# One fixed instruction order for the attention units of a hybrid attention and linear-attention block

## The chip, the cores and the metric

One core of a Trainium2 chip runs the whole kernel in one launch. The metric is the device time in microseconds (us). TensorE (PE) multiplies and transposes into PSUM; VectorE (DVE), ScalarE (ACT) and GpSimd (POOL) do the elementwise work; SyncE (SP) and here also ACT issue DMAs. The program lists each engine's instructions in an order of its own, and semaphores hold an instruction until what it needs is there.

## The reference

One layer of an encoder, 512 positions by 2048 channels in float32:

```python
mod = silu(c) @ w_cond + b_cond;  shift, scale, gate = split(mod, 3)
proj = (rms_norm(x) * (1 + scale) + shift) @ w_in       # 2048 x 7200
aq, ak, av, ag, gq, gk, gv, gg, lr_f, lr_b = split(proj)
a_out = attention(aq, ak, av) * silu(ag)   # 16 heads x 64, three dilated windows + bias, merged
g_o = gla(gq, gk, gv, log_g_f) + flip(gla(flipped, log_g_b))   # 4 heads, dk 128, dv 256
g_out = rms_norm(g_o) * gain * silu(gg)
x = x + gate * (concat(a_out, g_out) @ w_out)
return rms_norm(x) * final_gain
```

The kernel computes the three windows of a head as one softmax over all 512 keys, with a bias row that holds mask, multiplicity and relative position.

## The kernel before

A float32 operand is split into a high part (rounded to float32r, by ACT) and a low part (the difference, by DVE); `three` makes a product of three float32r matmuls (hi*hi, hi*lo, lo*hi). So every group of weights costs one ACT and one DVE pass over 128x1024 before PE can use it (`split_hi`, `split_lo`; the tiles are named qk42h and qk42l for group 2 of unit qk4).

The input projection runs in units of 512 columns: first two that are planned together with the loading of the inputs (sa, sb), then qk2, qk4, qk6 (queries and keys of head pairs 2 to 7), gk, gv0, gv1, ag0, ag1, gg0, gg1, and the output projection o0 to o3. A unit has 8 groups of weights; for each it makes 6 matmuls for each of its four tiles, 24 in all, into four PSUM banks of the pool `pj` (5 banks; the other three, pool `pa`, serve scores, transposes and values). A "tick" is 3 matmuls, a unit has 64. Beside the matmuls a unit carries side work: a list of (place, function), where the place is a share of the unit's ticks; what lies at 1 or above goes to the next unit at its place less one ("spill").

In qk2, qk4, qk6 and gk the side work is the attention of two head pairs whose queries and keys were made one unit earlier: 16 tiles (4 heads by 4 blocks of 128 queries), each of them
- `score`: two matmuls into s, then on DVE p = min with the bias and the row's extreme (`tensor_tensor_reduce`, L580), on ACT the exponential with the row's sum (L583), on DVE the reciprocal (L584), on POOL the scaling (L585);
- `turn`: four PE transposes of p into t, then ACT's high part (L601) and DVE's low part (L602) into pt;
- `values`, for every two tiles: eight matmuls of pt with v into o, an ACT copy oh and a DVE addition into cat.

The places are spread evenly from 0.17 over 0.8 of the unit (`ATT_AT`), transposes behind the score of two tiles later. After a unit `qk_evict` takes the new queries and keys out of the four banks, for each pair: ACT writes qs and ks, DVE their low parts (qs, kl), and SP copies ks and kl to the other 64 partitions by DMA.

PE's order is the order of the source (`manual_schedule(engines={E.PE})`). The other engines' instructions are ordered by the framework's scheduler from its own estimates, except in the start, where the block that plans the inputs lists them (`PLANNED`). In some units DVE also does "half sums" (`some_sums`, L244 and L680: 1024 columns of a weight matrix with one row, from a 512 KB load), as many as `SUMS_IN` says. Weight loads, half-sum loads and bias loads (`g_load`) all go over SP's queue. The names raw, rawv and rawg stand for loads that share four buffers.

Of the kernel before, what the change touches and what calls it, by code (L numbers as in the profile page):

```python
# [18 lines left out]
P = 128  # L19
# [114 lines left out]
def block_kernel(ctx: ExitStack, tc: tile.TileContext, a: dict):  # L134
# [15 lines left out]
    def B8(name, shape, dt=F32):  # L150
        return b8.tile([P] + shape, dt, tag="b8", name=name)
# [140 lines left out]
    def split_lo(i):  # L292
        if i in raws and i not in low:
            u, g = groups[i]
            raw = raws[i].rearrange("p k c -> p (k c)")
            hi, lo = wts[i]
            tt(lo, raw, hi.bitcast(F32), op=ALU.subtract)
            low.add(i)
# [257 lines left out]
    def attention(pairs):  # L556

        tiles = [(2 * p + j, i) for p in pairs for j in range(2) for i in range(4)]
        gt, pt, pr_ = {}, {}, {}
        heads = [2 * p + j for p in pairs for j in range(2)]  # L560

        def g_load(h):
            g = gp.tile([P, 896], F32, tag="g", name=f"g{h}")
            nc.sync.dma_start(g, bass.AP(grow.tensor, grow.offset + h * 1024, [[1, P], [1, 896]]))
            gt[h] = g

        def score(h, i):
            def go():
                if h % 8 == 0 and i == 0:
                    cat[h // 8] = B8(f"cat{h // 8}", [4, 512])  # L570
# [5 lines left out]
                mm(ps, qs[:, q], ks, start=True, stop=False)  # L576
                mm(ps, qs[:, q], kl, start=False, stop=True)  # L577
                t = T2(f"p{h}{i}")
                st = sm.tile([P, 3], F32, tag="st", name=f"st{h}{i}", bufs=6)
                nc.vector.tensor_tensor_reduce(  # L580
                    out=t, in0=ps, in1=gt[h][:, P * i:P * i + 512], op0=ALU.add, op1=ALU.min,
                    scale=1.0, scalar=3e38, accum_out=st[:, 0:1])
                act(t, t, AF.Exp, bias=st[:, 0:1], scale=-1.0, accum_out=st[:, 1:2])  # L583
                nc.vector.reciprocal(st[:, 2:3], st[:, 1:2])  # L584
                nc.gpsimd.tensor_scalar(t, t, st[:, 2:3], 1.0, op0=ALU.mult, op1=ALU.mult)  # L585
                pr_[h, i] = t
            return go

        def turn(h, i):
            def go():  # L590
                half, ii = divmod(i, 2)
                if ii == 0:
                    pt[h, half] = B8(f"pt{h}{half}", [2, 4, 256], F32R)
                t = pr_.pop((h, i))
                pk = PA(f"t{h}{i}")
                for kt in range(4):
                    nc.tensor.transpose(pk[:, kt * P:kt * P + P], t[:, kt * P:kt * P + P], ident)  # L597
                hi = pt[h, half][:, 0, :, P * ii:P * ii + P]
                lo = pt[h, half][:, 1, :, P * ii:P * ii + P]
                src = pk.rearrange("p (k q) -> p k q", k=4)  # L600
                act(hi, src, AF.Copy)  # L601
                tt(lo, src, hi.bitcast(F32), op=ALU.subtract)  # L602
            return go

        def values(h, half):
            def go():
                t = pt.pop((h, half))
                po = PA(f"o{h}{half}")
                for kt in range(4):
                    for w in range(2):  # L610
                        mm(po[:, :256], vv[h // 4][:, kt, h % 4, :], t[:, w, kt, :],  # L611
                           start=kt == 0 and w == 0, stop=kt == 3 and w == 1)
# [10 lines left out]
        for x in range(n + 4):  # L623
            if x < n:
                items.append(score(*tiles[x]))
            if 2 <= x <= n + 1:
                items.append(turn(*tiles[x - 2]))
            if 3 <= x <= n + 2 and tiles[x - 3][1] % 2 == 1:
                items.append(values(tiles[x - 3][0], tiles[x - 3][1] // 2))
        g_load(heads[0])  # L630
        start, span, move0, move1, move_last = ATT_AT
        at = [start + (q + 0.5) / len(items) * span for q in range(len(items))]
        at[0] -= move0
        at[1] -= move1
        at[-1] += move_last
        return list(zip(at, items))

    def gate_half(m, z):

# [203 lines left out]
    def unit(name, natural, side=(), rhs=None, lr=None, tiles=range(4)):  # L843
# [5 lines left out]
        for q in range(KT // 2):  # L849
            g = gorder[q] if name == "o3" else q  # L850
            i0 = gi[name, g]
            todo = []
            if 0 in tiles:
                todo = list(range(gi[name, gorder[0] if name == "o3" else 0], upto[name, g] + 1))
                for i in todo:
                    split_hi(i)
                for ahead in (1, 2):
                    fetch(upto[name, g] + ahead)
            if i0 not in low:
                split_lo(i0)  # L860
            hi, lo = wts[i0]
            for n, i in enumerate(tiles):
                for kk in range(2):
                    k = 2 * g + kk
                    rh, rl = (h_hi[:, k, :], h_lo[:, k, :]) if rhs is None else rhs[k]
                    if natural:
                        t = slice(i * P, i * P + P)
                        cw = slice(kk * 512, kk * 512 + 512)
                        three(ps[n], rh[:, t], rl[:, t], hi[:, cw], lo[:, cw], q + kk == 0, q + kk == KT // 2)
                    else:  # L870
                        c = slice(kk * 512 + i * P, kk * 512 + i * P + P)
                        three(ps[n], hi[:, c], lo[:, c], rh, rl, q + kk == 0, q + kk == KT // 2)
                    tick += 1
                    if tick % (2 * len(tiles)) == 2:
                        for i_ in todo:
                            split_lo(i_)
                    while pos < len(side) and side[pos][0] * ticks <= tick:
                        urgent(side[pos][1])
                        pos += 1
                if lr is not None:  # L880
                    lr(4 * g + i)
            for i_ in todo:
                split_lo(i_)
        while pos < len(side):
# [12 lines left out]
        lnexp()  # L897


    for p in range(2):  # L900
        qk_evict(p, psb["b", 4 + 2 * p], psb["b", 5 + 2 * p])
    for n, p in (("qk2", 0), ("qk4", 2), ("qk6", 4)):
        ps = unit(n, False, attention((p, p + 1)) + ([(0.05, shift_row)] + some_sums(n) if p == 4 else []))
        for q in range(2):
            qk_evict(p + 2 + q, ps[2 * q], ps[2 * q + 1])

    ps = unit("gk", False, attention((6, 7)) + some_sums("gk"))
    gla["k"] = B8("gkt", [4, 512])
    for i in range(4):
        act(gla["k"][:, i, :], ps[i], AF.Copy)  # L910


    lrb = B8("lrb", [KT, 32])
    nc.sync.dma_start(lrb, a["w_lr"][0])
    lrs = B8("lrs", [KT, 2, 32], F32R)
    act(lrs[:, :, 0, :], lrb, AF.Copy)
    tt(lrs[:, :, 1, :], lrb, lrs[:, :, 0, :].bitcast(F32), op=ALU.subtract)
    plr = PA("plr")

    def lr_tick(n):  # L920
        if n % 2 == 1:
            k = n // 2
            w = lrs[:, k, :, :].rearrange("p a b -> p (a b)")
            mm(plr[:64], w, h_hi[:, k, :], start=k == 0, stop=False)
            mm(plr[:64], w, h_lo[:, k, :], start=False, stop=k == KT - 1)

    ps = unit("gv0", True, some_sums("gv0"), lr=lr_tick)
    gla["v0"] = B8("gv0", [4, 512])
    for i in range(4):
        act(gla["v0"][:, i, :], ps[i], AF.Copy)  # L930
# [200 lines left out]
```

## Time and profile before

| | |
|---|---|
| three runs | 958.09, 958.55, 958.55 us; median 958.55 |
| the profiled execution | 959.9 us; its span (first to last instruction) 957.9 us |
| granted TensorE clock | 0.997 |
| busy | PE 98%, DVE 63%, ACT 45%, POOL 8% of the span |
| stage of the four attention units | about 192 to 460 us |

A line of instructions reads: start, duration, engine, source line, operation, what it writes and reads, and in brackets the engine's idle time before it and what ended it. Matmuls overlap, so the pace is the distance of their starts. A line of waits reads: who waited for whom, us in total, times, longest.

### The profile page before, as it was taken

The page shows a single profiled execution, that of the slowest core. Times are in us where ns is not written, and L with a number is a line of the kernel's source. Part 1 is how long each engine was busy: PE and PEld are TensorE (multiplying, and loading weights), DVE is VectorE, ACT ScalarE, POOL GpSimd, SP SyncE. Part 2 cuts the span into 40 slices and gives each one's busy share as a digit, 9 for nine tenths or more (in the row PEclk, how much of TensorE's full clock was granted, in tenths as well). Part 3 has the DMA queues.
Part 4 walks back from the last instruction along what each step waited for, and adds up shares of the span by engine and source line. Part 5 has one row for each costly group of instructions (what it writes and reads, how often), then busy time and mean ns, then how long its engine had stood idle before and what let it go on. Part 6 is the DMA issues. An engine that isn't in the chain of part 4 may idle for free.

```text
span 957.9 us, 11999 instructions
## 1 busy us (share of the span) xinstructions
PE 939.7 (98%) x4464; PEld 777.1 (81%) x4464; DVE 605.3 (63%) x900; ACT 431.5 (45%) x719; POOL 81.1 (8%) x100
## 2 busy tenths in 40 slices
PE   8999999999999999999999999999999999999996
PEld 5888788888888888888778888888887888888884
DVE  7988899675756676766435656675964352546421
ACT  5443533565655655655215544543834152233222
POOL 0000000012122022122000000000010000202120
PEclk9999999999999999999999999999999999999998
DMA  9999687443333463533454244354555464244013
GB/s 330 413 411 365 229 296 275 150 131 105 112 103 105 144 200 108 173 127 103 150 176 146 86 132 154 132 176 154 173 195 183 132 221 154 92 151 152 23 55 121
DMA packets 45180, 163.76 MB, mean 171 GB/s; under 512 B 5730, under 2 KB 6018, under 8 KB 40386
## 3 DMA queue, kind: packets, MB, share of 16 engines
q1 hardware_dynamic: 44946, 162.68, 49.9%
q8 instruction: 35, 0.57, 0.2%
q10 hardware_dynamic: 176, 0.33, 0.1%
q14 instruction: 23, 0.18, 0.1%
HBM read 154.51 MB, written 4.28 MB: 166 GB/s over the span
## 4 chain that ended last, share of the span: by engine, by line
PE 84%; DMA 6%; DVE 5%; issue 3%; ACT 1%; SPq 0%; POOL 0%; ACTq 0%; DVEq 0%; POOLq 0%
PE ps_o L170 6%; PE ps_o L169 6%; PE ps_o L171 6%; DMA rawg<-in_wg 6%; PE ps_qk L170 5%; PE ps_qk L169 5%; PE ps_qk L171 5%; PE o L611 3%; PE sta L169 3%; PE sta L170 3%; PE sta L171 3%; PE stb L171 3%; PE stb L169 3%; PE stb L170 3%; PE ps_gv L171 3%; PE ps_gv L170 3%
## 5 line engine op out<-in xcount | busy, mean ns | idle before, releaser
L585 POOL TENSOR_SCALAR p<-p,st 128x512 f32<-128x512 f32 x64 | 45.5, 711 | 406.6 <-DVE st L584 357.9
L244 DVE CUSTOM_DVE_ANT_0 cb<-cb,sb,c_bcond 128x2048 f32<-128x2048 f32 (+1 forms) x32 | 73.4, 2294 | 0.0
L583 ACT ACTIVATE p<-p,st 128x512 f32<-128x512 f32 x64 | 46.1, 721 | 56.8 <-DVE st L580 56.3
L602 DVE TENSOR_TENSOR pt<-t,pt 128x512 fp32r<-128x512 f32 x64 | 44.0, 689 | 16.2 <-ACT pt L601 15.8
L580 DVE CUSTOM_DVE_ANT_0 p<-s,g 128x512 f32<-128x512 f32 x64 | 43.6, 687 | 14.8 <-PE s L577 14.5
L601 ACT ACTIVATE pt<-t 128x512 fp32r<-128x512 f32 x64 | 37.8, 592 | 10.2 <-PE t L597 9.2
L244 DVE CUSTOM_DVE_ANT_0 rawg<-rawg,sb,gate 128x1024 f32<-128x1024 f32 x16 | 20.5, 1283 | 29.6 <-DMA rawg<-in_wg 29.6
L611 PEld LDWEIGHTS o<-pt,vv 128*128 128x128 f32 x256 | 34.7, 188 | 5.0 <-DVE pt L602 2.2
L597 PEld LDWEIGHTS t<-c_ident,p 128*128 128x128 f32 x256 | 31.8, 140 | 8.5
L597 PE MATMUL t<-c_ident,p 128*128 128x128 f32 x256 | 38.3, 272 | 0.0
L611 PE MATMUL o<-pt,vv 128*128 128x256 f32 x256 | 36.6, 283 | 0.9 <-DVE pt L602 0.8
L244 DVE CUSTOM_DVE_ANT_0 rawg<-rawg,sb,c_bcond 128x1024 f32<-128x1024 f32 x16 | 20.5, 1283 | 26.3 <-DMA rawg<-in_wg 26.3
L1014 POOL TENSOR_TENSOR x<-x,fgain 128x512 f32<-128x512 f32 x12 | 20.3, 1696 | 185.3 <-ACT ysq L1012 185.3
L1012 ACT ACTIVATE ysq<-x 128x512 f32<-128x512 f32 x16 | 10.1, 632 | 47.2 <-DVE x L1010 47.2
L767 POOL TENSOR_SCALAR dc<-st,sc 128x256 f32<-128x256 f32 x16 | 10.4, 652 | 245.5 <-DVE st L764 240.6
L1009 DVE TENSOR_TENSOR y<-ps_o,sb 128x512 f32<-128x512 f32 x16 | 10.9, 684 | 25.9 <-PE ps_o L171 25.9
L584 DVE RECIPROCAL st<-st 128x1 f32<-128x1 f32 x64 | 10.3, 162 | 24.9 <-ACT p L583 24.9
L576 PE MATMUL s<-ks,qs 128*128 128x512 f32 x64 | 25.1, 391 | 0.0
L577 PE MATMUL s<-kl,qs 128*128 128x512 f32 x64 | 25.0, 391 | 0.0
L774 ACT ACTIVATE sq<-st,sc 128x256 f32<-128x256 f32 x24 | 12.2, 509 | 26.8 <-DVE st L769 14.3
L1010 DVE TENSOR_TENSOR x<-y,x 128x512 f32<-128x512 f32 x16 | 18.0, 1125 | 0.3
L614 ACT ACTIVATE oh<-o 64x256 f32<-64x256 f32 x32 | 12.2, 382 | 13.0 <-PE o L611 12.2
(1275 smaller groups left out, 2916.7 us busy)
## 6 DMA issues: line engine op xcount, KB each, us to landing
cb<-in_wm SPq DMA_DIRECT2D x31, 1024.0 KB, 7.9
rawg<-in_wg SPq DMA_DIRECT2D x32, 512.0 KB, 3.4
raw_o<-in_w_o SPq DMA_DIRECT2D x32, 512.0 KB, 3.4
raw_qk<-in_w_qk SPq DMA_DIRECT2D x24, 512.0 KB, 3.4
rawb<-in_w_sb SPq DMA_DIRECT2D x16, 512.0 KB, 4.8
rawv<-in_wv SPq DMA_DIRECT2D x16, 512.0 KB, 3.8
raw_gv<-in_w_gv SPq DMA_DIRECT2D x16, 512.0 KB, 3.5
raw_ag<-in_w_ag SPq DMA_DIRECT2D x16, 512.0 KB, 3.3
```

Of the source, the lines that this page charges most:

```text
L169: mm(ps, lh, rh, start=first, stop=False)
L170: mm(ps, ll, rh, start=False, stop=False)
L171: mm(ps, lh, rl, start=False, stop=last)
L244: nc.vector.tensor_tensor_reduce(out=w, in0=w, in1=with_, op0=ALU.mult, op1=ALU.add, scale=1.0, scalar=init, accum_out=dst)
L576: mm(ps, qs[:, q], ks, start=True, stop=False)
L580: nc.vector.tensor_tensor_reduce(out=t, in0=ps, in1=gt[h][:, P * i:P * i + 512], op0=ALU.add, op1=ALU.min, scale=1.0, scalar=3e38, accum_o ...
L583: act(t, t, AF.Exp, bias=st[:, 0:1], scale=-1.0, accum_out=st[:, 1:2])
L585: nc.gpsimd.tensor_scalar(t, t, st[:, 2:3], 1.0, op0=ALU.mult, op1=ALU.mult)
L597: nc.tensor.transpose(pk[:, kt * P:kt * P + P], t[:, kt * P:kt * P + P], ident)
L601: act(hi, src, AF.Copy)
L602: tt(lo, src, hi.bitcast(F32), op=ALU.subtract)
L611: mm(po[:, :256], vv[h // 4][:, kt, h % 4, :], t[:, w, kt, :], start=kt == 0 and w == 0, stop=kt == 3 and w == 1)
```

## The change

Four things change, and with them the order on all engines.

1. From the start of qk2 to the end of gv0 the order of DVE, ACT, POOL and SP is that of the source as well (`manual_schedule(engines=PLANNED)`).
2. The attention's places: tile x's score at 0.12 + 0.057x, its reciprocal and scaling 0.75 tiles later, its transposes at 1.8 and every second tile's values at 2.9 tiles behind its score. The last tiles' transposes and values fall at 1.02 to 1.14 of the unit, so they spill into the next. (The new functions for transposes by DVE and a way through HBM, `turn`, `leave`, `back`, `part_hi`, `part_lo`, are not used, `BY_DVE` being empty; `pe_turn` is the old `turn`.)
3. In qk4, qk6 and gk the first two groups of weights form one step: 12 matmuls for a bank before the next bank. The groups needed for that are split one unit ahead, in the last step of the unit before.
4. Weight loads of qk and gk units (from the fourth on) and bias loads go over ACT's queue; the half sums of qk6 and gk move to later units; the split of the lr weights moves from the start of gv0 into gk.

```diff
-ATT_AT = (0.17, 0.8, 0.04, 0.05, 0.05)
+ATT_AT = (0.12, 0.057)
+BY_DVE = ()
-SUMS_IN = {"qk6": 4, "gk": 4, "gv0": 9, "gv1": 2, "ag0": 7, "ag1": 9, "gg0": 9}
+SUMS_IN = {"gv0": 12, "gv1": 5, "ag0": 8, "ag1": 9, "gg0": 9}
...
-            nc.sync.dma_start(raws[i], a["w_" + u][g])
+            queue = nc.scalar if u[:2] in ("qk", "gk") and i > 2 else nc.sync
+            queue.dma_start(raws[i], a["w_" + u][g])
...
-            nc.sync.dma_start(g, bass.AP(grow.tensor, grow.offset + h * 1024, [[1, P], [1, 896]]))
+            nc.scalar.dma_start(g, bass.AP(grow.tensor, grow.offset + h * 1024, [[1, P], [1, 896]]))
...
+        def scale(h, i):
+            def go():
+                t, st = pr_.pop((h, i))
                 nc.vector.reciprocal(st[:, 2:3], st[:, 1:2])
                 nc.gpsimd.tensor_scalar(t, t, st[:, 2:3], 1.0, op0=ALU.mult, op1=ALU.mult)
                 pr_[h, i] = t
             return go
...
+        for x in range(n):
+            h, i = tiles[x]
+            items.append((x, score(h, i)))
+            items.append((x + 0.75, scale(h, i)))
...
+                items.append((x + 1.8, pe_turn(h, i)))
+                if ii:
+                    items.append((x + 2.9, values(h, half)))
+        items.sort(key=lambda v: v[0])
         g_load(heads[0])
+        start, step = ATT_AT
+        return [(start + step * x, go) for x, go in items]
...
+        steps = [order_[:2]] if name in ("qk4", "qk6", "gk") else [order_[:1], order_[1:2]]
+        for step in steps + [[g] for g in order_[2:]]:
             todo = []
             if 0 in tiles:
+                end = upto[name, step[-1]] + (name[:2] == "qk" and step[-1] == order_[-1])
+                todo = list(range(gi[name, order_[0]], end + 1))
                 for i in todo:
                     split_hi(i)
                 for ahead in (1, 2):
+                    fetch(end + ahead)
+            for g in step:
+                split_lo(gi[name, g])
...
+    with tc.manual_schedule(engines=PLANNED):
...
+        for n, p in (("qk2", 0), ("qk4", 2), ("qk6", 4)):
+            ps = unit(n, False, attention((p, p + 1)) + ([(0.6, shift_row)] if p == 4 else []))
+            for q in range(2):
+                qk_evict(p + 2 + q, ps[2 * q], ps[2 * q + 1])
```

The order at the border of qk2 and qk4 (that to qk6 and that to gk look alike). On DVE before, from the split of group 1 of qk4; st_2037 is the last tile's row sum (L584 its reciprocal), L602 are low parts of transposed tiles, L540 and L550 the eviction:

```order
L297 TENSOR_TENSOR qk41l<-raw_qk_1961,qk41h 128x1024
L584 RECIPROCAL st_2037<-st_2037 128x1
L602 TENSOR_TENSOR pt_2004<-t_2050,pt_2004 128x4x128
L540 SCALAR_TENSOR_TENSOR qs_2106<-ps_qk_0_1509,qs_2106 64x512
L602 TENSOR_TENSOR pt_2061<-t_2062,pt_2061 128x4x128
L540 SCALAR_TENSOR_TENSOR qs_2109<-ps_qk_0_1509,qs_2109 64x512
L618 TENSOR_TENSOR cat_1549<-o_2072,oh_2081 64x256
L550 TENSOR_TENSOR kl_2113<-ps_qk_1_1510,ks_2112 64x512
L602 TENSOR_TENSOR pt_2061<-t_2090,pt_2061 128x4x128
```

On DVE now, from the same split; st_2078 is the last tile's row sum (L594 its reciprocal):

```order
L302 TENSOR_TENSOR qk41l<-raw_qk_1932,qk41h 128x1024
L545 SCALAR_TENSOR_TENSOR qs_2085<-ps_qk_0_1513,qs_2085 64x512
L545 SCALAR_TENSOR_TENSOR qs_2088<-ps_qk_0_1513,qs_2088 64x512
L555 TENSOR_TENSOR kl_2092<-ps_qk_1_1514,ks_2091 64x512
L555 TENSOR_TENSOR kl_2098<-ps_qk_1_1514,ks_2097 64x512
L545 SCALAR_TENSOR_TENSOR qs_2103<-ps_qk_2_1515,qs_2103 64x512
L545 SCALAR_TENSOR_TENSOR qs_2106<-ps_qk_2_1515,qs_2106 64x512
L555 TENSOR_TENSOR kl_2110<-ps_qk_3_1516,ks_2109 64x512
L555 TENSOR_TENSOR kl_2116<-ps_qk_3_1516,ks_2115 64x512
L302 TENSOR_TENSOR qk42l<-raw_qk_2010,qk42h 128x1024
L594 RECIPROCAL st_2078<-st_2078 128x1
```

The last tile's reciprocal moved from ahead of the eviction to behind it and behind one more split.

On PE before, the last tile's transposes (p_2036) and the border, where ps_qk_0_2144 begins:

```order
L597 MATMUL t_2090<-c_ident,p_2036 128x128 x4
L169 MATMUL ps_qk_2_1511<-h_hi,qk27h 128x512
L170 MATMUL ps_qk_2_1511<-h_hi,qk27l 128x512
L171 MATMUL ps_qk_2_1511<-h_lo,qk27h 128x512
L169 MATMUL ps_qk_3_1512<-h_hi,qk27h 128x512
L170 MATMUL ps_qk_3_1512<-h_hi,qk27l 128x512
L171 MATMUL ps_qk_3_1512<-h_lo,qk27h 128x512
L169 MATMUL ps_qk_3_1512<-h_hi,qk27h 128x512
L170 MATMUL ps_qk_3_1512<-h_hi,qk27l 128x512
L171 MATMUL ps_qk_3_1512<-h_lo,qk27h 128x512
L169 MATMUL ps_qk_0_2144<-h_hi,qk40h 128x512
```

On PE now, from the seventh instruction behind the border (ps_qk_0_2123 began six matmuls earlier); p_2049 is the last tile but one, p_2077 the last:

```order
L608 MATMUL t_2142<-c_ident,p_2049 128x128 x4
L665 MATMUL o_2149<-pt_2026,vv_921 128x256 x8
L173 MATMUL ps_qk_0_2123<-h_hi,qk41h 128x512
L174 MATMUL ps_qk_0_2123<-h_hi,qk41l 128x512
L175 MATMUL ps_qk_0_2123<-h_lo,qk41h 128x512
L173 MATMUL ps_qk_0_2123<-h_hi,qk41h 128x512
L174 MATMUL ps_qk_0_2123<-h_hi,qk41l 128x512
L175 MATMUL ps_qk_0_2123<-h_lo,qk41h 128x512
L173 MATMUL ps_qk_1_2124<-h_hi,qk40h 128x512
L174 MATMUL ps_qk_1_2124<-h_hi,qk40l 128x512
L175 MATMUL ps_qk_1_2124<-h_lo,qk40h 128x512
L608 MATMUL t_2170<-c_ident,p_2077 128x128 x4
```

The last two tiles' transposes moved from ahead of the border to behind it. The last score now stands three matmuls ahead of the border; before, the whole last group of weights stood between the two.

More of the change, by code (lines that the diff above doesn't have):

```diff
@@ L597, in go @@
                     nc.tensor.transpose(pk[:, kt * P:kt * P + P], t[:, kt * P:kt * P + P], ident)
-                hi = pt[h, half][:, 0, :, P * ii:P * ii + P]
-                lo = pt[h, half][:, 1, :, P * ii:P * ii + P]
+                hi, lo = [pt[h, half][:, e, :, P * ii:P * ii + P] for e in range(2)]
                 src = pk.rearrange("p (k q) -> p k q", k=4)
@@ L622, in attention @@
         n = len(tiles)
[L623 to L629, printed above, removed]
-        g_load(heads[0])
[L631 to L636, printed above, removed]
+        for x in range(n):
+            h, i = tiles[x]
+            items.append((x, score(h, i)))
+            items.append((x + 0.75, scale(h, i)))
+            half, ii = divmod(i, 2)
+            if half in BY_DVE:
+                items.append((x + 1.1, turn(h, i)))
+                items.append((x + 1.5, leave(h, i)))
+                if ii:
+                    for at, piece in zip(BACK_AT, (back, part_hi, part_lo, values)):
+                        items.append((x + at, piece(h, half)))
+            else:
+                items.append((x + 1.8, pe_turn(h, i)))
+                if ii:
+                    items.append((x + 2.9, values(h, half)))
+        items.sort(key=lambda v: v[0])
+        g_load(heads[0])
+        start, step = ATT_AT
+        return [(start + step * x, go) for x, go in items]
     def gate_half(m, z):
@@ L857, in unit @@
                 for ahead in (1, 2):
[L858 to L861, printed above, removed]
+                    fetch(end + ahead)
+            for g in step:
+                split_lo(gi[name, g])
             for n, i in enumerate(tiles):
[L863 to L881, printed above, removed]
@@ new lines, in unit @@
+                for g in step:
+                    hi, lo = wts[gi[name, g]]
+                    for kk in range(2):
+                        k = 2 * g + kk
+                        rh, rl = (h_hi[:, k, :], h_lo[:, k, :]) if rhs is None else rhs[k]
+                        first, last = (g, kk) == (order_[0], 0), (g, kk) == (order_[-1], 1)
+                        if natural:
+                            t = slice(i * P, i * P + P)
+                            cw = slice(kk * 512, kk * 512 + 512)
+                            three(ps[n], rh[:, t], rl[:, t], hi[:, cw], lo[:, cw], first, last)
+                        else:
+                            c = slice(kk * 512 + i * P, kk * 512 + i * P + P)
+                            three(ps[n], hi[:, c], lo[:, c], rh, rl, first, last)
+                        tick += 1
+                        if tick % (2 * len(tiles)) == 2:
+                            for i_ in todo:
+                                if i_ <= upto[name, step[-1]]:
+                                    split_lo(i_)
+                        while pos < len(side) and side[pos][0] * ticks <= tick:
+                            urgent(side[pos][1])
+                            pos += 1
+                    if lr is not None:
+                        lr(4 * g + i)
@@ L897, in gate_evict @@
         lnexp()
[L900 to L910, printed above, removed]
@@ L913, in block_kernel @@
[L913 to L925, printed above, removed]
@@ L927, in block_kernel, with lr_load, lr_part, lr_tick @@
-    ps = unit("gv0", True, some_sums("gv0"), lr=lr_tick)
+    with tc.manual_schedule(engines=PLANNED):
+        for i in range(3):
+            fetch(i)
+        split(0)
+        for p in range(2):
+            qk_evict(p, psb["b", 4 + 2 * p], psb["b", 5 + 2 * p])
+        for n, p in (("qk2", 0), ("qk4", 2), ("qk6", 4)):
+            ps = unit(n, False, attention((p, p + 1)) + ([(0.6, shift_row)] if p == 4 else []))
+            for q in range(2):
+                qk_evict(p + 2 + q, ps[2 * q], ps[2 * q + 1])
+        lrt2, lrs = [], []
+        def lr_load():
+            lrt2.append(T2("lrb").rearrange("p (k c) -> p k c", k=KT))
+            nc.scalar.dma_start(lrt2[0], a["w_lr"][0])
+        def lr_part(e):
+            lrs.append(T2(f"lrs{e}", F32R).rearrange("p (k e c) -> p k e c", k=8, e=2))
+            src = lrt2[0][:, 8 * e:8 * e + 8, :]
+            act(lrs[e][:, :, 0, :], src, AF.Copy)
+            tt(lrs[e][:, :, 1, :], src, lrs[e][:, :, 0, :].bitcast(F32), op=ALU.subtract)
+        ps = unit("gk", False, attention((6, 7)) + [(0.7, lr_load), (0.85, lambda: lr_part(0)), (0.9, lambda: lr_part(1))])
+        gla["k"] = B8("gkt", [4, 512])
+        for i in range(4):
+            act(gla["k"][:, i, :], ps[i], AF.Copy)
+        plr = PA("plr")
+        def lr_tick(n):
+            if n % 2 == 1:
+                k = n // 2
+                w = lrs[k // 8][:, k % 8, :, :].rearrange("p a b -> p (a b)")
+                mm(plr[:64], w, h_hi[:, k, :], start=k == 0, stop=False)
+                mm(plr[:64], w, h_lo[:, k, :], start=False, stop=k == KT - 1)
+        ps = unit("gv0", True, some_sums("gv0"), lr=lr_tick)
```

50 lines of the change are left out of this document (42 added, 8 removed).

## The prediction

> **What bounds the kernel now.** I read the page first: busy times, then the chain of waits.
>
> ```profile
> PE 939.7 (98%) x4464; PEld 777.1 (81%) x4464; DVE 605.3 (63%) x900; ACT 431.5 (45%) x719; POOL 81.1 (8%) x100
> PE 84%; DMA 6%; DVE 5%; issue 3%; ACT 1%; SPq 0%; POOL 0%; ACTq 0%; DVEq 0%; POOLq 0%
> ```
>
> TensorE (PE) is busy 98% of the span and carries 84% of the chain. Matmul ends are modelled, so I asked where PE waited:
>
> ```profile
> PE pc L238 <- ACT c L236: 3.4, 1, 3.4
> PE o L611 <- DVE pt L602: 0.8, 1, 0.8
> PE plr L924 <- DVE lrs L917: 0.4, 1, 0.4
> 250.00:300.00 50.00, 49.97 (x267) 42.07 (x266) 32.66 (x68) 29.22 (x56) 7.75 (x12) 1.00 0.38 113
> 450.00:500.00 50.00, 48.79 (x224) 38.56 (x223) 22.53 (x31) 13.09 (x19) 1.58 (x1) 1.00 0.51 163
> ```
>
> (The last two are windows: length, PE busy, its matmuls, then PEld, DVE, ACT, POOL, clock.) In 250 to 300, which holds the border from unit qk2 to qk4, PE idles 0.03 us; in 450 to 500, where gk ends, 1.21. The last two waits, 1.2 us, are all that the attention's part leaves to win. The change can hardly gain there. What it can do is make PE wait, so I went to the border of two units, PE first:
>
> ```profile
> 248.95 0.39 PE L577 MATMUL s<-kl,qs 128*128 128x512 f32 x1
> 249.18 0.39 PE L169 MATMUL ps_qk<-h_hi,qk27h 128*128 128x512 f32 x1
> 254.77 0.60 PE L597 MATMUL t<-c_ident,p 128*128 128x128 f32 x4
> 255.12 0.48 PE L169 MATMUL ps_qk<-h_hi,qk27h 128*128 128x512 f32 x1
> 255.44 0.40 PE L170 MATMUL ps_qk<-h_hi,qk27l 128*128 128x512 f32 x1
> 257.29 0.39 PE L169 MATMUL ps_qk<-h_hi,qk40h 128*128 128x512 f32 x1
> 257.97 1.12 PE L611 MATMUL o<-pt,vv 128*128 128x256 f32 x8
> 258.92 0.40 PE L169 MATMUL ps_qk<-h_hi,qk40h 128*128 128x512 f32 x1
> 264.39 0.39 PE L576 MATMUL s<-ks,qs 128*128 128x512 f32 x1
> ```
>
> The last tile's score (248.95) stands 8.3 us ahead of the border (257.29), its transposes (254.77) 2.5 us ahead, and the next score comes at 264.39. Matmuls start 0.23 us apart (248.95, 249.18); four transposes take 0.44 (254.77 to 255.44, less one 0.23); eight value matmuls 0.95 (257.97 to 258.92). In these 15 us between scores the eviction of the unit's projections (qs, ks, kl) runs on ACT and DVE, mixed with the last tiles' work, and PE waits for none of it.
>
> **The change part by part.** *1. The border.* By the order shown above, the last score now stands 3 matmuls ahead of the border (0.7 us), its transposes behind it: 15 matmuls, four transposes and eight value matmuls on, planned at 15 x 0.227 + 0.44 + 0.95 = 4.8 us. They need tile 15 scaled by POOL, POOL needs the reciprocal, and on DVE the reciprocal is behind qk41l, all eight eviction steps and qk42l. Before, it stood right behind qk41l. ACT likewise takes the eight evictions and qk42h after the last exponential. Durations:
>
> ```profile
> L539 ACT ACTIVATE qs<-ps_qk x12: 582/593/595, 251.6 to 392.2; 64x512 fp32r<-64x512 f32 x12
> L540 DVE SCALAR_TENSOR_TENSOR qs<-ps_qk,qs x12: 684/688/694, 252.4 to 393.4; 64x512 fp32r<-64x512 f32 x12
> L548 ACT ACTIVATE ks<-ps_qk x12: 592/592/597, 254.3 to 394.8; 64x512 fp32r<-64x512 f32 x12
> L550 DVE TENSOR_TENSOR kl<-ps_qk,ks x12: 683/688/696, 255.0 to 395.4; 64x512 fp32r<-64x512 f32 x12
> 190.02 0.59 ACT L539 ACTIVATE qs<-stb 64x512 fp32r<-64x512 f32 x1
> 190.65 0.68 DVE L540 SCALAR_TENSOR_TENSOR qs<-stb,qs 64x512 fp32r<-64x512 f32 x1 [1.71 <-ACT qs L539]
> 191.37 0.59 ACT L539 ACTIVATE qs<-stb 64x512 fp32r<-64x512 f32 x1 [0.75 <-DVE qs L540]
> 257.49 1.06 ACT L313 ACTIVATE qk42h<-raw_qk 128x1024 fp32r<-128x1024 f32 x1 [0.25 <-PE ps_qk L171]
> 258.58 1.23 DVE L297 TENSOR_TENSOR qk42l<-raw_qk,qk42h 128x1024 fp32r<-128x1024 f32 x1 [0.42 <-ACT qk42h L313]
> 249.49 0.69 DVE L580 CUSTOM_DVE_ANT_0 p<-s,g 128x512 f32<-128x512 f32 x1 [1.06 <-PE s L577]
> 250.22 0.73 ACT L583 ACTIVATE p<-p,st 128x512 f32<-128x512 f32 x1 [0.24 <-DVE st L580]
> 251.24 0.16 DVE L584 RECIPROCAL st<-st 128x1 f32<-128x1 f32 x1
> 251.56 0.70 POOL L585 TENSOR_SCALAR p<-p,st 128x512 f32<-128x512 f32 x1 [4.16 <-DVE st L584]
> ```
>
> The rows at 190 to 191 show that one bank's readers take turns, with 0.04 us from one engine to the other: ACT's second qs waits for DVE's first. So the evictions are a chain: five ACT steps (qs, qs, ks, qs, ks; the others are hidden) of 0.59, seven DVE steps of 0.69 up to the last ks, some nine passes of 0.04: 2.95 + 4.83 + 0.36 = 8.1 us. Ahead of it come the score's minimum 0.69 and the exponential 0.73 + 0.04; behind it qk42h 1.06, qk42l 1.23, the reciprocal 0.16, POOL 0.70, passes 0.2, and 0.2 for the bias load that ACT now issues: 3.55. In all 13.1 us from the start of that minimum. It can't start before the score ends, 0.5 us ahead of the border; DVE has tile 13's low part to do first, which waits for the transposes just ahead of the score, so I take 0.3 behind the border; two splits and two DMA issues on ACT in this last step could make it 1.1. Transposes at 13.4, planned at 4.8: PE waits 8.6 us, between 7.8 and 9.4. PE has nothing else to issue: behind the transposes stand all its matmuls. Three borders are built so (to qk4, qk6, gk): 25.8 us. The step meant as cover, two weight groups together on the unit's first bank, gives 12 matmuls before the second bank is needed, some 4.1 us with what stands between; that bank's two qs are out at about 4.4. It covers one bank's eviction nearly, not a chain of 13.
>
> *2. The clock behind such a wait.* No stall of this size is in the trace. After one of 1.24 us PE went on at 0.23 a matmul; after the empty start it did not:
>
> ```profile
> 724.85 0.49 PE L819 MATMUL gn<-gsh,ones 128*128 128x512 f32 x1 [1.24 <-ACT gsh L817]
> 726.14 0.39 PE L170 MATMUL ps_gg<-h_hi,gg07l 128*128 128x512 f32 x1
> 726.37 0.40 PE L171 MATMUL ps_gg<-h_lo,gg07h 128*128 128x512 f32 x1
> 14.12 0.63 PE L170 MATMUL sta<-sa0h,h_lo 128*128 128x512 f32 x1
> 14.55 0.63 PE L171 MATMUL sta<-sa0l,h_hi 128*128 128x512 f32 x1
> 12.00:16.00 4.00, 4.00 (x9) 2.82 (x10) 3.51 (x5) 1.62 (x3) 0.00 (x0) 1.00 1.02 412
> 16.00:20.00 4.00, 4.00 (x17) 3.22 (x16) 4.00 (x5) 2.43 (x4) 0.00 (x0) 1.00 1.01 407
> ```
>
> At 14 us they start 0.43 apart, 9 in 4 us, then 17. About 5 us at 0.43 are 12 matmuls with 0.2 lost on each, 2.4 us; the other end is nothing. PE was empty for 3.4 us there (the wait of pc above) and slow behind it, so eight idle microseconds are nearer to the start than to 1.24; I take 2.0 a border, 6.0 (0 to 7.2). [...]
>
> *3. The first unit.* No transposes spill into qk2, but the evictions of pairs 0 and 1 are a chain too. It starts at 190.02 as before, 1.85 us ahead of the unit's first matmul (191.87 in the same timeline), and ends 7.0 us after that. Then minimum 0.69, exponential 0.73, qk22h 1.06, qk22l 1.23 (both now ahead of the reciprocal), 0.16, 0.70, passes 0.25: 11.8. The first transposes stand behind 45 matmuls and two scores of two: 49 x 0.227, 11.1. A wait of 0.7, and about 0.3 at tile 2, which also has a split ahead of its reciprocal: 1.0 (0 to 2).
>
> *4. gk to gv0.* Here only four copies of 0.59 and one split stand between the last exponential and its reciprocal: 0.3 + 0.69 + 0.73 + 2.1 + 1.06 + 1.23 + 0.16 + 0.70 + 0.25 = 7.2, planned 5.3 (two more matmuls for lr): 1.9 of wait, in place of the 1.2 quoted above: +0.7 (-1.2 to +2).
>
> *5. Inside the units.* A tile's transposes follow its score by 20 matmuls, a score and a set of transposes: 5.4 us from its last start, 5.2 from its end. With a split in between the chain needs 0.4 + 0.69 + 0.73 + 1.06 + 1.23 + 0.16 + 0.70 + 0.2 = 5.2. I cost it at nothing; it is the second rival.
>
> *6. The rest.* Weight loads move from SP's queue to ACT's; they are issued two groups ahead as before, into slots freed a step earlier. Eight half sums of 1.28 us leave qk6 and gk; gv0, gv1 and gg1 take them. In gv0 DVE was busy under half (22.53 of 50): nothing, at most 1.5 either way where a sum's late load holds DVE in gv1 to gg1.
>
> Sum: 25.8 + 6.0 + 1.0 + 0.7 = 33.5 us. On the profiled execution's 959.9 that is 993.4; the runs' median, 958.55, is 1.35 lower, so I forecast 992. Low: 3 x 7.8 - 1.2 - 1.5, 979. High: 3 x 9.4 + 7.2 + 2 + 2 + 1.5, and 6 for part of 5: 1005.
>
> **The rivals.** *Faster:* the transposes at the border find their tile ready, and the fixed order only removes the 1.2 us at gk's end and perhaps that of 1.24 at 724. Time 956 to 957.4. It decides at 4.8 us: the reciprocal's chain would have to take that instead of 13.1, so the eviction steps would have to run side by side; the rows at 190 speak against it, and that ACT is idle 55% of the span does not help a chain. 0.05.
>
> *Waits in every step:* point 5 has no slack. If each of some 24 splits beside a score costs 0.5 to 1 us, 12 to 24 come on top: 1004 to 1016. For it: DVE now does all in one order. Against: most tiles have no split, and a delayed PE gives the others time. 0.12.
>
> *The bank covers it:* only some borders pay, because PE is late already where the chain begins; about 970. 0.03. *No change* because gains and stalls meet: 0.02.
>
> **How the numbers follow.** My forecast has 0.78. Its own range is 979 to 1005; to leave out no more than 2 in 10 it reaches to 976 below and 1012 above. A difference of 0.2%, 1.9 us, is about what a measurement can tell: faster 0.05, same 0.02, slower 0.93.
>
> **What would show it.** In the waits of PE, a line "PE t <- POOL p" with three waits of about 8 us, at the third slot of qk4, qk6 and gk; PE's idle time up by some 28 us, all between 200 and 500; after each, matmuls 0.43 apart; DVE and ACT alternating on qs, ks, kl ahead of each. Wrong: no such waits (the order isn't what holds PE), waits of under 5 us (evictions run side by side), full rate behind them (the clock), or many waits under 1 us all along the units (the second rival).

## The result, and the profile after

The changed kernel takes 995.52 us (median of four runs, 995.17 to 999.17) beside 958.32 for the kernel before: a ratio of 1.040, with a 95% interval from 1.0374 to 1.0427. It is slower, by 37 us. The profiled execution is the 999.17 one, with a span of 997.1 us, 39.2 more than before; it is the longest of the four, and the other three lie within 0.5 us of each other.

The busy line of the page and two lines of TensorE's waits (who waited for whom, us in total, times, longest):

```profile
PE 949.6 (95%) x4464; PEld 783.9 (79%) x4464; DVE 603.5 (61%) x901; ACT 430.7 (43%) x720; POOL 80.0 (8%) x100
PE t L608 <- POOL p L595: 29.5, 5, 7.8
PE kt L804 <- DVE ki L794: 1.9, 1, 1.9
```

The work has hardly changed (PE 4464 matmuls as before, DVE 603.5 us beside 605.3). Waits have come, and behind them a lower clock (0.980 granted over the span, 0.997 before), by which the same matmuls keep PE busy for 949.6 us in place of 939.7. One group has nearly all of the waits: transposes that wait for POOL's scaled tile, five times. Windows show where (length, PE busy and its matmuls, then PEld, DVE, ACT, POOL, the granted clock, with 1.00 for full, and the DMA engines' share and GB/s):

```profile
260.00:285.00 25.00, 17.24 (x84) 14.33 (x83) 13.62 (x25) 10.68 (x20) 2.08 (x3) 0.86 0.36 100
285.00:340.00 55.00, 55.00 (x293) 46.12 (x292) 30.61 (x71) 29.00 (x58) 9.75 (x14) 1.00 0.24 85
340.00:365.00 25.00, 17.24 (x78) 14.27 (x77) 11.37 (x22) 9.74 (x18) 2.08 (x3) 0.80 0.38 100
365.00:420.00 55.00, 55.00 (x297) 46.25 (x296) 31.81 (x71) 29.31 (x58) 9.08 (x13) 1.00 0.29 104
```

In the stretches between the borders TensorE never waits (55.00 of 55.00). At the borders to qk4, qk6 and gk it idles 7.76 us each, and the clock is below 1.00, because it is 0.50 for 6.83 or 10.24 us there ("half clock" from here on). The first border, on TensorE:

```profile
262.06 0.39 PE L580 MATMUL s<-kl,qs 128*128 128x512 f32 x1
262.98 0.40 PE L173 MATMUL ps_qk<-h_hi,qk40h 128*128 128x512 f32 x1
267.58 0.39 PE L175 MATMUL ps_qk<-h_lo,qk40h 128*128 128x512 f32 x1
275.73 1.12 PE L608 MATMUL t<-c_ident,p 128*128 128x128 f32 x4 [7.76 <-POOL p L595]
```

The same place on DVE and ACT:

```profile
262.71 0.68 DVE L583 CUSTOM_DVE_ANT_0 p<-s,g 128x512 f32<-128x512 f32 x1
263.44 0.73 ACT L586 ACTIVATE p<-p,st 128x512 f32<-128x512 f32 x1 [1.37 <-DVE st L583]
264.16 0.57 ACT L544 ACTIVATE qs<-ps_qk 64x512 fp32r<-64x512 f32 x1
271.81 0.59 ACT L553 ACTIVATE ks<-ps_qk 64x512 fp32r<-64x512 f32 x1 [0.92 <-DVE kl L555]
273.51 1.22 DVE L302 TENSOR_TENSOR qk42l<-raw_qk,qk42h 128x1024 fp32r<-128x1024 f32 x1 [0.39 <-ACT qk42h L318]
274.66 0.15 DVE L594 RECIPROCAL st<-st 128x1 f32<-128x1 f32 x1
```

The last tile's exponential is done at 264.2. Its reciprocal, a step of 0.15 us, starts 10.5 us later, behind the eviction (264.16 to 272.40 on ACT) and the split of group 2.

The start of qk2 waits too, for another reason (ACTq is ACT's DMA issue):

```profile
197.75 0.37 ACTq L569 DMA_DIRECT2D g<-grow  x1
203.28 0.69 DVE L583 CUSTOM_DVE_ANT_0 p<-s,g 128x512 f32<-128x512 f32 x1 [4.22 <-DMA g<-grow]
207.01 0.16 DVE L594 RECIPROCAL st<-st 128x1 f32<-128x1 f32 x1
208.10 1.11 PE L608 MATMUL t<-c_ident,p 128*128 128x128 f32 x4 [4.80 <-POOL p L595]
```

The first tile's minimum needs the bias g. That load stands in ACT's order behind the eviction and lands 5.5 us after its issue, and DVE sits idle for it.

### The profile page after: what moved, and what is told of

The parts are those of the page before. It is cut to its first block, busy times and chain, and to the rows that moved or that the text cites. A ratio compares the mean times of both kernels' runs of the same rounds, so it can differ in the third digit from the quotient of the medians.

```text
span 997.1 us, 11907 instructions
## 1 busy us (share of the span) xinstructions
PE 949.6 (95%) x4464; PEld 783.9 (79%) x4464; DVE 603.5 (61%) x901; ACT 430.7 (43%) x720; POOL 80.0 (8%) x100
## 5 line engine op out<-in xcount | busy, mean ns | idle before, releaser
L608 PE MATMUL t<-c_ident,p 128*128 128x128 f32 x256 | 40.9, 284 | 29.5 <-POOL p L595 29.5
L594 DVE RECIPROCAL st<-st 128x1 f32<-128x1 f32 x64 | 10.3, 161 | 31.9 <-ACT p L586 31.8
L672 DVE TENSOR_TENSOR cat<-o,oh 64x256 f32<-64x256 f32 x32 | 13.2, 414 | 10.3 <-ACT oh L668 9.7
```

## Experiments

**What stands behind the eviction.** First: is it the reciprocal alone, or all that spills?

```
# attention(), places of the scale
- items.append((x + 0.75, scale(h, i)))
+ items.append((x + (0.4 if x == n - 1 else 0.75), scale(h, i)))
```

> The changed kernel, with only the last tile's scale (reciprocal on DVE, product on POOL) given an earlier place, so that both stand ahead of the border. My theory (the whole of what spills over a border stands on DVE and ACT behind the eviction and the split of the next unit's third group): the wait 't <- POOL p' of 7.8 us at each of the three borders goes, and TensorE comes to the next spilled step: the next unit's first score needs the PSUM tile that the last but one tile's transposes hold until DVE's subtraction for pt, which stands behind eight eviction steps and a split, about 13 us after the border; a new wait 's <- DVE pt' of about 5.5 us there, and about 0.6 us for the first eviction, which starts later. So about 1.8 us less a border and up to 3 us of half clock less: 985 to 991 us. Rival A (the reciprocal alone is late, the rest has its cover): all three stalls go, 964 to 968. Rival B (the merged first step, or ScalarE's loads, hold the border up whatever the reciprocal does): 994 to 997.

Measured: 992.57 us, ratio 1.0364 (1.0347 to 1.0381). TensorE's waits:

```profile
PE s L579 <- DVE pt L612: 15.5, 3, 5.2
PE t L608 <- POOL p L595: 4.5, 1, 4.5
```

Three waits of 7.8 us have become three of 5.2, for the next spilled step: a score that needs the PSUM tile which the last but one tile's transposes hold until DVE has taken pt. Rival A falls, and so does B. The time is 1.6 us above my range. I had hoped for up to 3 us less of half clock, and it did not shrink: it lasts 6.83 us at each border, with 16 or 17 matmuls in it, where the changed kernel has 9, 16 and 11.

Second, the merged first step:

```
# unit()
- steps = [order_[:2]] if name in ("qk4", "qk6", "gk") else [order_[:1], order_[1:2]]
+ steps = [order_[:1], order_[1:2]]
```

> The changed kernel with the merged first step undone in the units qk4, qk6 and gk (each weight group is a step of its own again); places and fixed order stay. My theory: the split of the third group (1.2 us on DVE, 1.05 on ACT) is no longer ahead of the last tile's reciprocal, the rest of the chain is; each border's stall ends 1.2 to 1.7 us earlier, 989 to 993 us. Rival A (the merged step makes the stall): 964 to 972. Rival B (the merged step covers the eviction, and without it TensorE waits for banks as well): 998 to 1005.

Measured: 990.98 us, ratio 1.0351 (1.033 to 1.0372).

```profile
PE t L608 <- POOL p L595: 19.4, 5, 5.0
273.14 1.11 PE L608 MATMUL t<-c_ident,p 128*128 128x128 f32 x4 [4.34 <-POOL p L595]
PE ps_qk L173 <- DVE qs L545: 1.9, 2, 1.0
```

The wait at a border falls from 7.8 to 4.3 us (the one of 5.0 is that of qk2's start), and 1.0 us for a bank comes at each of the three (the last line has two of them; the third stands under gk). The merged step does cover the bank, and it puts one more split ahead of the reciprocal, which costs more. It isn't what makes the stall; both rivals fall.

Third, nothing spills:

```
- ATT_AT = (0.12, 0.057)
+ ATT_AT = (0.15, 0.0445)
```

> The changed kernel with its two numbers for the attention's places, 0.12 and 0.057, made 0.15 and 0.0445, so that the last step of a unit (values, at index 17.9) has the place 0.947 and nothing spills over the border. My theory: the three border stalls (7.9 us each, 23.8) and the half clock behind them (about 6) go, and the kernel has 965 to 968 us; what is left over before is the start of the second unit (5 us and the half clock), the 1.5 us ahead of gv0 and the 2 us in gv1. Rival A (the closer spacing makes TensorE wait in each tile, since the chain from score to transposes takes about 4 us of the 5.9 that it then has): 975 to 990. Rival B (the border is held up by the eviction itself or the merged first step): 985 to 997.

Measured: 983.63 us, ratio 1.0274 (1.0257 to 1.0291). I expected 965 to 968. The old wait was gone, and another stood under it. ACT, DVE and TensorE at the first border:

```profile
270.29 0.34 ACTq L569 DMA_DIRECT2D g<-grow  x1
275.88 0.69 DVE L583 CUSTOM_DVE_ANT_0 p<-s,g 128x512 f32<-128x512 f32 x1 [2.73 <-DMA g<-grow]
278.52 1.11 PE L608 MATMUL t<-c_ident,p 128*128 128x128 f32 x4 [4.34 <-POOL p L595]
```

It is the wait of qk2's start: g is issued behind the eviction and lands 5.6 us later. The first transposes of the new unit wait 4.3, 4.5 and 3.6 us. The time also lies in the range of rival A (the closer spacing makes each tile wait), but the trace speaks against it: all waits of transposes but those at the borders and at qk2's start make some 3 us. In the changed kernel g is issued at 271.89, but TensorE is late already and makes the score only at 279.67, so the load does not show there.

Fourth, the changed kernel without its fixed order:

```
- with tc.manual_schedule(engines=PLANNED):   # qk2 to gv0
+ if True:
```

> The changed kernel without the fixed order over the attention's units (the scheduler orders DVE, ACT, POOL and SP again there); places, merged step, loads on ScalarE's queue and sums stay. In its order the last tile's reciprocal stands behind one eviction step and one split in place of eight and two. My theory: the border stalls fall from 7.9 us to 0 to 2 us and bring no half clock, 962 to 973 us. Rival A (the places alone make the stall, whoever orders): 990 to 997. Rival B (the loads on ScalarE's queue make it): 990 to 997 too, and loads alone decide in a later run.

Measured: 975.03 us, ratio 1.0181 (1.016 to 1.0202), 2 us above my range and far from both rivals.

```profile
PE s L580 <- DMA kl<-kl: 6.1, 3, 2.2
PE s L579 <- DMA ks<-ks: 4.2, 3, 1.9
```

The wait of the transposes at the borders is gone. The 10.3 us that are left, with 3.4 lost to half clock behind them, I put down to the place: the first score, at 0.12, comes ahead of the copies of ks and kl that it reads (the run with the scheduler's order and later places, below, tests this). So the order costs some 20 us here, and 17 are left.

**The load under the first wait.** The table g is loaded one head ahead across borders as well:

```
# score()
- if i == 1 and h != heads[-1]:
+ if i == 1 and h < 15:
      g_load(h + 1)
# attention(); g_load itself and its table of loads move out of it
- g_load(heads[0])
# ahead of the first qk_evict
+ g_load(0)
```

> The changed kernel with the load of a unit's first table g issued ahead of the eviction at the unit's border (for the first unit ahead of the eviction at the end of sb; for the others from the last head's second score), still on ScalarE's queue. In the changed kernel's trace the start of qk2 waits 5 us: the score's mask step waits on DVE for g, which lands at 203.28, 1.9 us after the score. My theory: the start of qk2 gains those 1.9 to 2 us and up to 1.5 of half clock; the three borders keep their 7.9 us, since there the reciprocal comes later than g: 991 to 994 us. Rival A (g bounds the borders too): 965 to 980. Rival B (the start of qk2 waits for the split qk22 and not for g): 995 to 996.

Measured: 990.36 us, ratio 1.0327 (1.0312 to 1.0343), 0.6 below my range.

```profile
199.39 0.69 DVE L584 CUSTOM_DVE_ANT_0 p<-s,g 128x512 f32<-128x512 f32 x1
PE t L609 <- POOL p L596: 25.2, 5, 7.8
```

The minimum now follows the eviction's last step at once (198.66 + 0.69), and qk2's start waits 0.6 us in place of 4.8. The borders keep 7.8, so rival A is out. So g cost the start of qk2, and the spilled scale the borders.

Both edits together (places 0.15 and 0.0445, g ahead):

> The kernel with nothing spilled (places 0.15 and 0.0445; 983.6 us), with each unit's first g loaded ahead of the eviction as well. With nothing spilled each border still waited 4.0 to 4.9 us, now for the new unit's first transposes, whose mask step waited for g until 275.8 at the first border, 5.5 us after its issue behind the eviction on ScalarE's queue. My theory: with g there the mask step stands only behind the eviction and the split of qk42 on DVE, and the wait falls to about 1.8 us at each border and to under 1 at the start of qk2; the half clock, 3.4 to 6.8 us long at each border, mostly goes: 963 to 971 us. Rival (the eviction itself is what the border waits for): 979 to 985.

Measured: 969.40 us, ratio 1.0109 (1.0092 to 1.0125).

```profile
PE t L609 <- POOL p L596: 7.9, 11, 1.6
269.77 1.23 DVE L302 TENSOR_TENSOR qk42l<-raw_qk,qk42h 128x1024 fp32r<-128x1024 f32 x1 [0.39 <-ACT qk42h L318]
271.03 0.69 DVE L584 CUSTOM_DVE_ANT_0 p<-s,g 128x512 f32<-128x512 f32 x1
```

Together the two edits take away 26 us of the 37. At the border 1.6 us are left: the minimum stands behind qk42's split, whose product is needed later than the tile.

Is it the order alone? The kernel before, with nothing but the fixed order (places, steps, queues and sums its own):

```
- ...                                         # qk2 to gv0, as it was
+ with tc.manual_schedule(engines=PLANNED):
+     ...
```

> The kernel before, with only the fixed order (the engines DVE, ACT, POOL and SP take the source's order) over the same units; places, steps, sums and queues are those of before, whose reciprocal stands directly behind its exponential and does not spill. My theory, as the run with nothing spilled has extended it: the source's order puts the load of each unit's first g on SP behind the eight copies of the eviction, so it lands 13 us after the border, the first transposes wait about 4 us at each border and as much at qk2's start, with 2 us of half clock each, and the unmerged first step about 1 us for banks: 972 to 992 us. Rival (the fixed order costs nothing by itself; the spilled scale is all): 957 to 964.

Measured: 992.49 us, ratio 1.0349 (1.033 to 1.0368), 0.5 above the upper end. The rival is out: the source's order costs 34 us though no reciprocal spills. My account of it holds for qk2's start and fails at the borders. TensorE's waits are many:

```profile
PE t L597 <- POOL p L585: 5.1, 1, 5.1
PE o L611 <- DVE pt L602: 3.7, 8, 0.8
PE ps_qk L170 <- DVE qk41l L297: 1.5, 1, 1.5
282.92 0.60 PE L597 MATMUL t<-c_ident,p 128*128 128x128 f32 x4
279.15 0.69 DVE L580 CUSTOM_DVE_ANT_0 p<-s,g 128x512 f32<-128x512 f32 x1 [3.00 <-DMA g<-grow]
```

At qk2's start the first transposes wait 5.1 us for the chain behind g, as said. At the first border DVE does wait 3.0 us for g, but the transposes (282.92) do not wait: their place is late enough. There TensorE waits 0.5 us for a bank, 0.7 for qk41's high part and 1.5 for its low part, which stand behind the eviction, and the other two borders look alike. One more wait of 3.3 us comes in qk6, where DVE stands before a half sum whose row has not landed, and there are waits under 1 us for pt along the units. In all TensorE is idle for 24.6 us between 190 and 510 us, where the kernel before has 1.3, and half clock takes 3.4. The rest of the 34 us shows as no wait, and which of these waits the time hangs on was not tried.

**The other parts.** Three of gv1's five sums put into ag0:

```
- SUMS_IN = {"gv0": 12, "gv1": 5, "ag0": 8, ...}
+ SUMS_IN = {"gv0": 12, "gv1": 2, "ag0": 11, ...}
```

> The changed kernel with three of the five sums of gv1 (1.28 us each on DVE) put into ag0 instead, as many in gv1 as before the change. In the changed kernel's trace TensorE waits 2.0 us in gv1 at 573 us for DVE's product ki, behind a sum and a split that the kernel before does not have there, and runs 3.4 us at half clock after. My theory: this wait and its half clock go, 991 to 993.5 us. Rival (the order of the split, not the sum, makes the wait): 995 to 996.

Measured: 999.25 us, ratio 1.0426 (1.0407 to 1.0446): no gain on the changed kernel's 1.040 (1.0374 to 1.0427). The wait for ki is gone as expected; new ones came in ag0:

```profile
PE att L843 <- DVE st L828: 1.2, 2, 0.8
PE gn L879 <- DVE gsl L877: 0.8, 1, 0.8
```

My theory was right on the place and wrong on the time: the sums took their wait along. About 1 us of the 3.6 that I expected is not found in these lines; the two profiled spans, 997.2 and 997.1 us, are the same.

The loads back on SP's queue:

```
- queue = nc.scalar if u[:2] in ("qk", "gk") and i > 2 else nc.sync
+ queue = nc.sync
- nc.scalar.dma_start(g, ...)
+ nc.sync.dma_start(g, ...)
```

> The changed kernel with the loads of the weights and of g back on SP's queue, in the source's order. My theory: ScalarE's queue is not what the borders wait for (the reciprocal on DVE is, and g stays hidden behind it), so they keep 7.9 us; at the start of qk2 g would be issued on SP behind the eight copies of the eviction, about 2 us later than on ScalarE's queue, and the first transposes wait 7 us in place of 5: 996 to 1000 us. Rival (the issues on ScalarE's queue, 0.33 to 0.92 us each, delay its work and so every border): 975 to 990.

Measured: 998.68 us, ratio 1.0427 (1.0408 to 1.0445).

```profile
204.53 0.69 DVE L583 CUSTOM_DVE_ANT_0 p<-s,g 128x512 f32<-128x512 f32 x1 [5.09 <-DMA g<-grow]
```

In the range: the borders keep 7.8 us, so the rival is out, and g, issued at 199.98 behind SP's eight copies, lands 1.25 us later than on ACT's queue. The first transposes wait 5.7 us in place of 4.8, less than the 7 I expected. What matters is less the queue than what g stands behind.

All three cures by hand: nothing spills, g is ahead, and the split of the third group goes behind the first tile's scale. Against the run with both edits:

```
- ATT_AT = (0.15, 0.0445)
+ ATT_AT = (0.165, 0.0437)
# unit()
- if tick % (2 * len(tiles)) == 2:
+ if tick % (2 * len(tiles)) == 2 and len(step) == 1 or tick == 14 and len(step) == 2:
- "gv0": 12, "gv1": 5,
+ "gv0": 14, "gv1": 3,
```

> The kernel with nothing spilled and g ahead (969.4 us), with three edits more: the split of each merged unit's third group (1.23 us on DVE) behind the first tile's scale in place of ahead of its mask step; places 0.165 and 0.0437, so that the first transposes come one step of 0.68 us later; two of gv1's five sums in gv0. The fixed order, the merged step, the loads on ScalarE's queue and the transposes on TensorE stay. My theory: the 1.8 us left at each border fall to under 0.6, the second tile's 0.7 stays, the wait in gv1 (1.55 us) falls by 1.2: 960 to 966 us, so still not faster than the kernel before (958 to 959). Rival A (the eviction's eight steps alone set the first transposes): 967 to 970. Rival B (with the last large waits gone nothing of the change costs time): 955 to 958, faster than before.

Measured: 967.37 us, ratio 1.0099 (1.0082 to 1.0117), 1.4 above my range.

```profile
PE t L609 <- POOL p L596: 5.6, 7, 1.3
PE z L765 <- DVE ups L1020: 2.8, 1, 2.8
246.54 1.23 DVE L302 TENSOR_TENSOR qk27l<-raw_qk,qk27h 128x1024 fp32r<-128x1024 f32 x1 [1.83 <-ACT qk27h L318]
```

The time touches rival A's range (the eviction alone sets the first transposes), but the waits behind the borders are gone, so it is out. Others have come: 1.0 to 1.3 us near the end of each unit, where DVE waits for a split's high part with a ready reciprocal behind it, and 2.8 in gv1 for ups, behind the sums that I had moved.

The scheduler's order with places that don't spill:

```
- with tc.manual_schedule(engines=PLANNED):   # qk2 to gv0
+ if True:
- ATT_AT = (0.12, 0.057)
+ ATT_AT = (0.165, 0.0437)
```

> The changed kernel without the fixed order over the attention's units (975 us as it is) and with the places 0.165 and 0.0437, so that nothing spills. In that run TensorE waited at each border 2 to 4.4 us for the copies of ks and kl, which the first score at the place 0.12 comes to too early. My theory: the score comes three steps (2 us) later and the eviction has the spilled tile's steps no longer between its own, so these waits fall to 0 to 1.5 us and the kernel has 959 to 966 us: with the scheduler's order and with the source's order, mended by hand, about the same. Rival (the places cost nothing under the scheduler; its order delays the eviction anyway): 971 to 976.

Measured: 960.01 us, ratio 1.0025 (1.0015 to 1.0035).

```profile
PE t L608 <- POOL p L595: 1.7, 2, 1.3
```

So under the scheduler's order the merged step, the loads on ACT's queue, the moved sums and these places together cost 0.25%. The rest of the 4% is the fixed order and the places that spill.

Last, the moved sums in the kernel before:

```
- SUMS_IN = {"qk6": 4, "gk": 4, "gv0": 9, "gv1": 2, "ag0": 7, "ag1": 9, "gg0": 9}
+ SUMS_IN = {"qk6": 0, "gk": 3, "gv0": 12, "gv1": 2, "ag0": 8, "ag1": 9, "gg0": 9}
```

> The kernel before with only the sums placed anew: none in qk6, three in gk, twelve in gv0, two in gv1, and from there on as in the changed kernel. In the trace of before TensorE waits 1.9 us at 723 (gn, behind a sum on DVE whose rows land late); the changed kernel does not have that wait, and its own new one in gv1 comes with five sums there. My theory: the wait at gn goes with the new places of the sums, and with two sums in gv1 no wait comes there: 955.5 to 957.3 us beside some 957.3 to 958.8 for the kernel before, the one part of the change that is worth something. Rival (the wait at gn hangs on other parts, or comes up elsewhere): 957.5 to 960.

Measured: 958.42 us, ratio 1.0005 (0.9993 to 1.0017). I expected 955.5 to 957.3, and the rival's range holds. The wait at gn fell from 1.2 us (not 1.9, as I had it) to 0.4, too little to measure. No version here beats the kernel before.

## Why the prediction was right, point by point

The forecast of 992.0 lies 3.5 us below the median, and most of the time came for the reason that it gave: three waits of 7.8 us at the borders with half clock behind them, and TensorE's idle time up by 29 us (28 forecast). That it came so near is in part luck: one term was 6.7 us too small, and the borders, 2.5 too large, took back some of it.

- **The border (8.6 us each, measured 7.76).** The chain was right, its parts to within some 0.2 us: 13.0 us from the start of the minimum (262.71) to the transposes (275.73), with 13.1 worked out, and the transposes were due 4.8 us behind the border, as planned. What was off is the start: I put the minimum 0.3 us behind the border, and it came 0.27 ahead of it. That is 0.57 of the 0.84 us. The three borders cost 23.3 in place of 25.8. The 0.2 us in that chain for the issue of the bias load is shown by no run: the issue took 0.34 us (271.89) beside the last copy of ks, and qk42h began at 272.43, 0.03 behind that copy. The early scale shows one thing that the prediction left out: the chain holds all that spilled, so with the reciprocal out of it the next spilled step still waits 5.2 us.
- **The clock (6.0 us).** Behind the first wait 9 matmuls took the 2.99 us in which TensorE was busy at a granted clock of 0.50:

```profile
268.48:271.89 3.41, 0.00 (x0) 0.00 (x0) 2.45 (x4) 1.54 (x4) 0.00 (x0) 1.00 0.53 117
271.89:278.72 6.83, 2.99 (x9) 2.57 (x10) 3.79 (x6) 3.14 (x5) 0.69 (x1) 0.50 0.80 219
278.72:282.13 3.41, 3.41 (x20) 2.98 (x19) 0.70 (x2) 0.94 (x3) 0.00 (x0) 1.00 0.01 4
```

  The matmuls start 0.43 us apart there, as forecast:

```profile
277.07 0.63 PE L174 MATMUL ps_qk<-h_hi,qk40l 128*128 128x512 f32 x1
277.50 0.63 PE L175 MATMUL ps_qk<-h_lo,qk40h 128*128 128x512 f32 x1
```

  Half of the busy time at half clock is lost (0.43 us a matmul in place of 0.23). In the half clock behind the three waits TensorE was busy 2.99, 5.87 and 3.87 us, since it lasts 6.83 or 10.24 us and begins at a different distance from the wait's end: 6.4 us in all. It starts at 207.02, 271.88, 346.97 and 425.48, whole multiples of 3.413 us apart.
- **The first unit (1.0 us, measured 4.8 of wait and 2.9 of half clock).** This is the step that failed. I followed the eviction's chain and not the load of g, which the fixed order puts behind that eviction; the point on loads that move to ACT's queue spoke of weights alone. With g ahead the wait is 0.6 us, beside the 0.7 that I had for it.
- **gk to gv0 (+0.7).** A wait of 1.4 us in place of 1.2: +0.2. (Four copies of 0.59 us would make 2.36, not the 2.1 of the forecast's sum; in the trace they overlap and take 2.04.)
- **Inside the units (0).** Right: 55.00 of 55.00 us busy in the two stretches shown. The second rival is out.
- **The rest (0, at most 1.5).** Too narrow: the wait for ki in gv1 is 1.9 us and brings 1.7 of half clock (half of 3.41 us); against it the wait at 724, 1.4 us in both its parts, is gone.

The sum: 23.3 + 6.4 + 7.7 + 0.2 + 2.2 = 39.8, and the two profiled spans differ by 39.2. The medians differ by 37.2; where the other executions save the 2 us was not traced.

## What to carry to other kernels

An order that is written by hand decides for every instruction what it stands behind, and a 0.15 us reciprocal or a load's issue that stands behind an eviction pays the whole eviction (the reciprocal came 10.5 us behind its exponential, DVE waited 4.2 us for the load). So where side work may spill over a border, list for each engine, in its order, all that is emitted at the border ahead of the spilled steps and ahead of the first steps of the new unit, DMA issues included, and follow each one to TensorE. When one such wait goes, expect the next one under it: here they were the spilled scale, the pt behind it, the bias load and the split of a later group, in that order.

## What the runs showed of the hardware

In one place half clock followed on a wait of 1.88 us. In the changed kernel's trace it comes with five waits: it starts at the four times given above, and in gv1 at 575.66, 368.64 us or 108 times 3.413 behind the first. Ahead of this last start TensorE was idle for 1.88 of 3.41 us, by the busy times that the trace gives. In the run with the scheduler's order it was idle for 1.76 of 3.42 us, and the clock stayed at 1.00. The two places, the changed kernel first:

```profile
572.25:575.66 3.41, 1.53 (x8) 0.96 (x7) 2.78 (x5) 2.77 (x7) 0.00 (x0) 1.00 0.41 132
575.66:579.08 3.42, 3.42 (x10) 2.82 (x10) 2.09 (x4) 0.98 (x2) 0.36 (x1) 0.50 0.69 228
```

```profile
339.24:342.66 3.42, 1.66 (x10) 1.48 (x11) 0.00 (x0) 0.00 (x0) 0.00 (x0) 1.00 0.60 132
342.66:346.07 3.41, 3.41 (x19) 2.88 (x18) 2.19 (x5) 1.31 (x3) 0.00 (x0) 1.00 0.18 38
```

So the wait in gv1 cost 1.7 us more, and the idle time in the second example nothing. What decides between the two was not shown. Half clock lasted longer where TensorE was idle inside it: 3.41 us in gv1, where it was busy throughout, 6.83 at the start of qk2 and at the first and third border with 1.08, 3.84 and 2.96 us idle, and 10.24 at the second border with 4.37.
